# Top-4-of-32 expert layer: results scaled by slot weights and added to a sum in HBM by accumulating scatters; 16 separate slot tables; x joined by products in the last tiles

## The chip, the cores and the metric

One core of one Trainium2 chip runs the whole layer in one launch. The core has TensorE (PE; PEld is its weight load), VectorE (DVE), ScalarE (ACT), GpSimd (POOL) and SyncE (SP). The metric is the device time of one execution in microseconds, the median of several runs.

## The reference

The layer ends in a mixture of experts over 512 latent tokens of 1024 channels. Four of 32 experts are chosen per token and their results are added with softmax weights:

```python
logits = (xf @ lp['router_w'] + lp['router_b']).astype(jnp.float32)
top_v, top_e = lax.top_k(logits, TOP_K)              # TOP_K = 4 of 32
weights = jax.nn.softmax(top_v, axis=-1)
...
gate = xblk @ lp['exp_w_gate'][e] + lp['exp_b_gate'][e]
up = xblk @ lp['exp_w_up'][e] + lp['exp_b_up'][e]
return clamped_swiglu(gate, up) @ lp['exp_w_down'][e] + lp['exp_b_down'][e]
...
contrib = yb[dest] * sorted_w[:, None].astype(yb.dtype)
out = jax.ops.segment_sum(contrib, sorted_tok, num_segments=n_tok)
```

The sum is scaled by a row of modulation values (`ga2`), added to the residual x, and the result goes through a last RMSNorm. All is float32. Before the experts stand the adaLN norm, the input projection, the RWKV and gating branches and their merge; the change leaves these alone but for some instructions that its order puts among them.

## The kernel before

Float32 precision is reached by splitting each operand into a high part (a cast) and a low part (the rest), with three products for one. An expert's three matrices of 1024 x 1024 come in twelve loads of 1 MB (`expert_raw`, on SP, six buffers named raw). ACT casts each to wh (`whigh`), DVE subtracts to wl (`wlow`), and PE runs twelve products of 512 columns on it (`block`). `expert_chain` (line 1625 on) writes this order out by hand for PE, ACT and DVE: per expert r there are 12 positions: 0 to 3 the gate matrix of r, 4 to 7 the down matrix of expert r-1, 8 to 11 the up matrix of r. At each position the cast of the block three further on and the subtraction of the block two further on are written first. SP and POOL take their instructions in the order of the program's text as their scheduler finds them ready.

An expert has 128 slots, about half of them used (512 tokens x 4 / 32 experts = 64 on average). The rows of experts 0 to 3 (`NMM = 4`) are picked by products with one-hot matrices (`gather_x`, two experts at a time: 64 products of 256 columns on PE, 16 casts on ACT). For the later ones `x_rows` gathers 128 rows by an indirect DMA whose list is a column of `slots`, and `x_turn` transposes them. `slots` comes from one table `d_tab` in HBM: `slot_table` sends 16 indirect DMAs from POOL, one per token tile and choice, each of 128 numbers of 4 bytes, all into the same table; then the table is read back. `side` runs this next to expert 0, a piece at each position.

`y_out` (line 1575) copies the expert's result from PSUM to the tile am (one buffer, shared with the next expert's activations) and writes 128 rows to `d_y` from ACT. After the last expert `finish` gathers 16 tiles of rows from `d_y`, and for each token tile adds two of them by products with diagonal weights on PE, the down biases by one more product, the last expert's rows by a one-hot product with `wT`, and two by DVE; then multiplies by `ga2`, adds x, and normalises.

Of the kernel before, what the change touches and what calls it, by code (L numbers as in the profile page):

```python
# [31 lines left out]
NMM = 4  # L32
# [19 lines left out]
NLATE = C_IOTA1 + 128  # L52
# [14 lines left out]
def make_consts():  # L67
# [41 lines left out]
    l[:, C_EB:C_EB + 32] = 1024.0 * np.arange(32)  # L109
    hst = np.zeros((40, 512), np.float32)  # L110
# [41 lines left out]
class K:  # L152
# [1168 lines left out]
    def scratch(self, *shape):  # L1321

        t = self.mraw.tile([128, 2048], F32, name="raw", bufs=RAW)
        n = math.prod(shape)
        names = "abcd"[:len(shape)]
        return t[:, :n].rearrange(f"p ({' '.join(names)}) -> p {' '.join(names)}", **dict(zip(names, shape)))

    def weights(self, pool):
# [7 lines left out]
        yield  # L1336
# [5 lines left out]
        yield  # L1342
        eb = self.late[:, C_EB:C_EB + 32]
        pe = moe.tile([128, 4, 32], F32, name="pe")
        nc.vector.tensor_add(pe, self.pos, eb.rearrange("p (a e) -> p a e", a=1).to_broadcast([128, 4, 32]))
        dst = moe.tile([128, 4, 4], F32, name="dst")
        t = self.scratch(4, 4, 32)
        nc.vector.tensor_mul(t, oh, pe.rearrange("p a (b e) -> p a b e", b=1).to_broadcast([128, 4, 4, 32]))
        nc.vector.tensor_reduce(dst, t, axis=mybir.AxisListType.X, op=OP.add)
        yield  # L1350
        e_ = moe.tile([128, 4, 4], F32, name="dse")
        t = self.scratch(4, 4, 32)
        nc.vector.tensor_mul(t, oh, eb.rearrange("p (a b e) -> p a b e", a=1, b=1).to_broadcast([128, 4, 4, 32]))
# [9 lines left out]
        nc.vector.scalar_tensor_tensor(s, e_, 0.125, f, op0=OP.mult, op1=OP.add)  # L1363
        self.slot = pool.tile([128, 4, 4], I32, name="slot")
        nc.vector.scalar_tensor_tensor(self.slot, big, 8192.0, s, op0=OP.mult, op1=OP.add)
        self.slot_table(pool)
        self.f_, self.e_, self.big = f, e_, big

    def weights_end(self, pool):
# [4 lines left out]
        f, e_, big = self.f_, self.e_, self.big  # L1374
        self.keepR = self.mbL.tile([128, 4096], F32R, name="mL")
        self.keep = self.mb.tile([128, 4096], F32, name="mH")
        wl = moe.tile([128, 4, 4], F32, name="ex")
        nc.vector.tensor_mul(wl, self.wts, oh[:, :, :, NE - 1])
        self.wlast = pool.tile([128, 4, 1], F32, name="wlast")
        nc.vector.tensor_reduce(self.wlast.rearrange("p a b -> p (a b)"), wl, axis=mybir.AxisListType.X, op=OP.add)  # L1380
        yield
        yield from self.down_bias(pool, oh)
        yield
        self.wts2 = pool.tile([128, 4, 4], F32, name="wts2")
        nc.vector.tensor_mul(self.wts2, self.wts, big)
        nc.vector.tensor_sub(self.wts, self.wts, self.wts2)
        yield
        g = moe.tile([128, 4, 4], F32, name="dst")
        nc.vector.tensor_scalar_min(g, f, 127.0)
        self.dsti = pool.tile([128, 4, 4], I32, name="dsti")  # L1390
        nc.vector.scalar_tensor_tensor(g, e_, 0.125, g, op0=OP.mult, op1=OP.add)

        nc.vector.tensor_scalar_min(self.dsti, g, 128.0 * (NE - 1))
        nc.vector.tensor_scalar(g, f, 128.0, -128.0, op0=OP.max, op1=OP.add)
        self.dst2 = pool.tile([128, 4, 4], I32, name="dst2")
        nc.vector.scalar_tensor_tensor(self.dst2, e_, 0.375, g, op0=OP.mult, op1=OP.add)

    def slot_table(self, pool):

        nc = self.nc  # L1400
        tok = pool.tile([128, 4], I32, name="tok")
        lt = self.late[:, C_TOK:C_TOK + 12].rearrange("p (i c) -> p i c", c=3)
        nc.vector.tensor_add(tok.rearrange("p (i c) -> p i c", c=1), lt[:, :, 0:1], lt[:, :, 1:2])
        for i in range(4):
            for k in range(4):
                nc.gpsimd.indirect_dma_start(out=self.d_tab, out_offset=bass.IndirectOffsetOnAxis(ap=self.slot[:, i, k:k + 1], axis=0),  # L1406
                                             in_=tok[:, i:i + 1], in_offset=None, bounds_check=128 * NE - 1, oob_is_err=False)
# [3 lines left out]
    def down_bias(self, pool, oh):  # L1411

        nc = self.nc
        moe = self.moe
        w = self.scratch(4, 3, 32)
        u = self.scratch(4, 4, 32)
# [8 lines left out]
        self.wD = self.keepR[0:96, 0:512].rearrange("p (a b) -> p a b", a=4)  # L1425
        nc.scalar.copy(self.wD, pt)
        nc.vector.tensor_sub(self.wD[32:64], pt[32:64], self.wD[32:64])
        b = self.mraw.tile([96, 2048], F32, name="raw", bufs=RAW)[:, :1024]
        for j in range(3):
            nc.sync.dma_start(b[32 * j:32 * j + 32, :], self.A["exp_b_down"])  # L1430
        yield
        self.bD = self.keepR[0:96, 512:1536]
        nc.scalar.copy(self.bD, b)
        nc.vector.tensor_sub(self.bD[64:96], b[64:96], self.bD[64:96])
# [82 lines left out]
    def x_rows(self, e):  # L1517

        t = self.xg[e] = self.moex.tile([128, 1024], F32, name="xg", bufs=2)
        self.nc.gpsimd.indirect_dma_start(out=t, out_offset=None, in_=self.d_h2, in_offset=bass.IndirectOffsetOnAxis(ap=self.slots[:, e:e + 1], axis=0))  # L1520
# [54 lines left out]
    def y_out(self, E):  # L1575
        y = E["y"] = self.moe.tile([128, 1024], F32, name="am")
        self.nc.scalar.copy(y, E["dn"].rearrange("p a b -> p (a b)"))
        if E["e"] < NE - 1:
            self.nc.scalar.dma_start(self.d_y[128 * E["e"]:128 * E["e"] + 128, :], y)

    def expert_bias(self, tmp, m):
# [20 lines left out]
        zi = tmp.tile([128, 32], I32, name="zi", bufs=1)  # L1602
        nc.gpsimd.memset(zi, 0)
        nc.sync.dma_start(self.d_tab.rearrange("(p e) a -> p (e a)", p=128), zi)

    def experts(self):
# [3 lines left out]
        with self.tc.manual_schedule(engines={ET.PE, ET.Activation, ET.DVE}):  # L1610
            y = self.expert_chain()
        self.finish(y)

    def side(self):

        self.counts(self.small)
        yield
        yield from self.weights(self.small)

    def side_end(self):  # L1620

        yield from self.weights_end(self.small)
        yield from self.last_table()

    def expert_chain(self):
# [29 lines left out]
        gather, side, side_end = iter(()), self.side(), self.side_end()  # L1655
        for i, (r, e, n, pos) in enumerate(seq):
# [5 lines left out]
            if pos == 0 and r % 2 == 1 and r + 1 < NMM:  # L1662
                gather = self.gather_x((r + 1) // 2, xT)

            if pos == 0:
                X = xT.pop(r)
                E["gp"] = ps.tile([128, 2, 512], F32, name="gp", bufs=1)
                if NMM <= r + 2 < NE:
# [9 lines left out]
            elif pos == 4:  # L1678
                P["dn"] = ps.tile([128, 2, 512], F32, name="dn", bufs=1)
                if r == NE:  # L1680
# [4 lines left out]
                    self.up_half(P, 1)  # L1685
            elif pos == (5 if P else 9) and E:
# [22 lines left out]
            if r == 1:  # L1709
                next(gather, None)  # L1710
            next(side if r < 2 else side_end, None)
        self.y_out(P)
        return P["y"]

    def last_table(self):

        nc = self.nc
        z = self.mraw.tile([128, 2048], F32, name="raw", bufs=RAW)[0:1, :1024]
        nc.vector.memset(z, 0.0)
        nc.scalar.dma_start(self.d_y[128 * (NE - 1):128 * (NE - 1) + 1, :], z)  # L1720
        oh = self.scratch(4, 128)
# [25 lines left out]
    def finish(self, y):  # L1747

        nc = self.nc
        yg = {}  # L1750
        for i in range(4):
            for k in range(4):
                if k % 2 == 0:
                    t = self.mraw.tile([128, 2, 1024], F32, name="raw", bufs=RAW)
                yg[i, k] = t[:, k % 2, :]
                nc.gpsimd.indirect_dma_start(out=yg[i, k], out_offset=None, in_=self.d_y, in_offset=bass.IndirectOffsetOnAxis(ap=self.dsti[:, i, k:k + 1], axis=0))
# [292 lines left out]
```

## Time and profile before

| what | value |
|---|---|
| median of 3 runs | 2066.53 us (2059.87 to 2074.01) |
| the profiled execution | 2061.29 us, span 2059.5 us, mean granted TensorE clock 0.964 |
| busy share | PE 95%, DVE 80%, ACT 60%, POOL 16% |
| first block of expert 0 on PE | 830.5 us after the span's start |
| last product of expert 31 | ends at about 2022.5 us |

The span runs from the first to the last instruction of the profiled execution; 1.8 us of its time lie around it. The profiled execution is 5.2 us below the median of the runs. Three stretches matter here: the merge and router up to 821 us, the experts to 2022 us, and the finish. A row of the timeline gives start, duration, engine, line, operation, output<-input; in brackets stands the time the engine sat idle before it, and what released it.

### The profile page before, as it was taken

The numbers are of one execution on the slowest core, as the hardware profiler recorded it, in microseconds if no ns is written. First come the engines' busy times: TensorE is split into PE (matmuls) and PEld (weight loads), VectorE is DVE, ScalarE is ACT, GpSimd is POOL, SyncE is SP. The second block draws the span as 40 slices with busy tenths as digits, with TensorE's granted clock in tenths as the row PEclk, the third lists the DMA queues.
The fourth block names the chain that finished last, engine by engine and source line by source line (L and its number), as shares of the span: only waits on it lengthen the run. The fifth ranks groups of instructions, "written<-read, shape, count | busy, mean of one in ns | idle before, by whom it ended". The sixth has DMA issues, their size and how long they took to land.

```text
span 2059.5 us, 29236 instructions
## 1 busy us (share of the span) xinstructions
PE 1950.5 (95%) x11344; PEld 1523.6 (74%) x11344; DVE 1657.3 (80%) x1760; ACT 1228.1 (60%) x1400; POOL 328.0 (16%) x362
## 2 busy tenths in 40 slices
PE   7999889989999998987999999999999999999986
PEld 4767666766666678876888888888888888888863
DVE  5755876867766367886899999999999999999985
ACT  4522534343534234775777777777777777777762
POOL 0001605343423353122000000000000000000013
PEclk9999988989979998998999999999999999999998
DMA  9666232111112185788999999999999999999994
GB/s 313 210 207 194 62 120 78 45 59 37 46 42 69 39 264 213 292 280 337 355 380 374 390 374 385 371 379 379 373 391 372 382 379 380 379 372 394 362 342 171
DMA packets 154675, 545.11 MB, mean 265 GB/s; under 512 B 14442, under 2 KB 75626, under 8 KB 105379
## 3 DMA queue, kind: packets, MB, share of 16 engines
q1 hardware_dynamic: 140775, 497.97, 65.2%
q0 software_dynamic: 6928, 23.10, 3.3%
q10 hardware_dynamic: 6828, 22.13, 2.7%
q8 instruction: 91, 1.49, 0.3%
q14 instruction: 53, 0.43, 0.1%
HBM read 507.71 MB, written 35.43 MB: 264 GB/s over the span
## 4 chain that ended last, share of the span: by engine, by line
PE 67%; issue 7%; DVE 6%; POOL 3%; DMA 2%; ACT 1%; SPq 0%; POOLq 0%; DVEq 0%; ACTq 0%
PE dn L1490 5%; PE dn L1486 5%; PE dn L1485 5%; PE up L1485 5%; PE gp L1485 5%; PE gp L1486 5%; PE up L1486 5%; PE up L1490 5%; PE gp L1490 5%; PE fill L1079 4%; PE ch L906 1%; PE b L1568 1%; PE mm L865 1%; PE b L1532 1%; POOL d_tab L1406 1%
## 5 line engine op out<-in xcount | busy, mean ns | idle before, releaser
L1474 DVE TENSOR_TENSOR wl<-raw,wh 128x2048 fp32r<-128x2048 f32 x384 | 869.2, 2292 | 52.1 <-PE gp L1490 28.7
L1468 ACT CAST wh<-raw 128x2048 fp32r<-128x2048 f32 x384 | 720.5, 1905 | 96.2 <-PE gp L1486 60.5
L1485 PE MATMUL dn<-wh,aH 128*128 128x512 f32 x512 | 207.6, 406 | 0.4 <-ACT aH L1571 0.4
L1485 PE MATMUL gp<-wh,xH 128*128 128x512 f32 x512 | 204.7, 400 | 0.0
L1485 PE MATMUL up<-wh,xH 128*128 128x512 f32 x512 | 204.5, 399 | 0.0
L1486 PE MATMUL dn<-wh,aL 128*128 128x512 f32 x512 | 202.3, 395 | 1.5 <-DVE aL L1572 1.3
L1486 PE MATMUL gp<-wh,xL 128*128 128x512 f32 x512 | 201.9, 394 | 0.0
L1486 PE MATMUL up<-wh,xL 128*128 128x512 f32 x512 | 201.8, 394 | 0.0
L1520 POOL DMA_INDIRECT xg<-d_h,slots x28 | 26.3, 940 | 898.8 <-PE b L1532 889.4
L1490 PE MATMUL dn<-wl,aH 128*128 128x512 f32 x512 | 140.2, 395 | 0.0
L1490 PE MATMUL up<-wl,xH 128*128 128x512 f32 x512 | 139.2, 393 | 0.0
L1490 PE MATMUL gp<-wl,xH 128*128 128x512 f32 x512 | 139.0, 393 | 0.0
L1571 ACT CAST aH<-b 128x512 fp32r<-128x512 f32 x64 | 37.5, 587 | 133.6 <-PE b L1568 133.6
L1486 PEld LDWEIGHTS dn<-wh,aL 128*128 128x128 f32 x512 | 97.3, 190 | 22.0 <-DVE aL L1572 2.9
L1490 PEld LDWEIGHTS gp<-wl,xH 128*128 128x128 f32 x512 | 96.2, 188 | 22.9
L1490 PEld LDWEIGHTS up<-wl,xH 128*128 128x128 f32 x512 | 96.1, 188 | 22.9
L1486 PEld LDWEIGHTS up<-wh,xL 128*128 128x128 f32 x512 | 96.6, 189 | 21.3
L1490 PEld LDWEIGHTS dn<-wl,aH 128*128 128x128 f32 x512 | 96.6, 189 | 21.2
L1485 PEld LDWEIGHTS dn<-wh,aH 128*128 128x128 f32 x512 | 97.3, 190 | 20.2 <-ACT aH L1571 0.8
L1486 PEld LDWEIGHTS gp<-wh,xL 128*128 128x128 f32 x512 | 96.6, 189 | 21.1
L1485 PEld LDWEIGHTS gp<-wh,xH 128*128 128x128 f32 x512 | 96.4, 188 | 20.7
L1485 PEld LDWEIGHTS up<-wh,xH 128*128 128x128 f32 x512 | 96.4, 188 | 20.7
(510 smaller groups left out, 3753.2 us busy)
## 6 DMA issues: line engine op xcount, KB each, us to landing
raw<-in_exp_w_gate_dram SPq DMA_DIRECT2D x128, 1024.0 KB, 7.2
raw<-in_exp_w_up_dram SPq DMA_DIRECT2D x128, 1024.0 KB, 7.9
raw<-in_exp_w_down_dram SPq DMA_DIRECT2D x128, 1024.0 KB, 9.3
raw<-in_w_ada_dram SPq DMA_DIRECT2D x32, 512.0 KB, 4.5
d_y<-am ACTq DMA_DIRECT2D x31, 512.0 KB, 8.8
raw<-in_w_in_dram SPq DMA_DIRECT2D x24, 512.0 KB, 4.0
wa<-in_w_ada_dram SPq DMA_DIRECT2D x7, 1024.0 KB, 11.7
raw<-in_w_in_dram SPq DMA_DIRECT2D x6, 1024.0 KB, 5.3
```

What stands on the lines that cost most here:

```text
L865: nc.tensor.matmul(mm[:, par, d, :], BK[r, d, ch[d], :], AR[r, d, ch[d], :], start=True, stop=True)
L906: nc.tensor.matmul(sp[:, d, :], bk[:, d, :], uv[:, d, :], start=True, stop=True)
L1079: nc.tensor.matmul(ps, a[:, k, :], b[:, k, :], start=(n == 0), stop=(n == 23))
L1406: nc.gpsimd.indirect_dma_start(out=self.d_tab, out_offset=bass.IndirectOffsetOnAxis(ap=self.slot[:, i, k:k + 1], axis=0), in_=tok[:, i:i + ...
L1468: self.nc.scalar.copy(h, t)
L1474: self.nc.vector.tensor_sub(lo, t, h)
L1485: mm(ps[:, c, :], xH[:, k0 + kk, :], wh[:, cs], start=first and kk == 0, stop=False)
L1486: mm(ps[:, c, :], xL[:, k0 + kk, :], wh[:, cs], start=False, stop=False)
L1490: mm(ps[:, c, :], xH[:, k0 + kk, :], wl[:, cs], start=False, stop=last and kk == 1)
L1520: self.nc.gpsimd.indirect_dma_start(out=t, out_offset=None, in_=self.d_h2, in_offset=bass.IndirectOffsetOnAxis(ap=self.slots[:, e:e + 1], ...
L1532: nc.tensor.transpose(pt[:, j, :], self.xg[e][:, 128 * k:128 * k + 128], self.ident)
L1571: nc.scalar.copy(aH, pt)
```

## The change

Each slot now has a row of two numbers, token + 1 and weight. `places` computes slots and weights at once, ahead of the first two subtractions, and sends 16 indirect DMAs into 16 separate tables; SP and ACT load these in turn, eight each, and `slot_rows` adds them up. The tables are zeroed by 16 POOL DMAs in `expert_bias`; before, one SP DMA did it. `NMM` is 2: experts 2 and 3 are gathered by DMA. `x_rows` skips slots without a token (a bound on the index). `sum_start` writes the weighted down biases to a sum `d_acc` in HBM; `y_out` scales the expert's rows by the slot weights on ACT and adds them to `d_acc` by an indirect DMA with an addition, from POOL; unused slots go to 128 spare rows. `sum_load` reads the sum back after expert 30, `x_sum` adds it to x at the last positions, and `finish` joins x by a product with the unit matrix and the last expert by `wT`, in the hand-written order.

```diff
-NMM = 4
+NMM = 2
+    def places(self, pool):
...            (softmax weights wts, slot number slot, tw = [token + 1, weight])
+        for i in range(4):
+            for k in range(4):
+                nc.gpsimd.indirect_dma_start(out=self.d_tab[4 * i + k], out_offset=bass.IndirectOffsetOnAxis(ap=slot[:, i, k:k + 1], axis=0),
+                                             in_=tw[:, i, k, :], in_offset=None, bounds_check=128 * NE - 1, oob_is_err=False)
+        self.tab = moe.tile([128, 16, NE, 2], F32, name="am")
+        for j, t in enumerate(self.d_tab):
+            (nc.sync, nc.scalar)[j % 2].dma_start(self.tab[:, j], t.rearrange("(s e) a -> s e a", e=NE))
+    def slot_rows(self, pool):
+        v = moe.tile([128, NE, 2], F32, name="slv")
+        nc.vector.tensor_reduce(v, self.tab.rearrange("p j e a -> p e a j"), axis=mybir.AxisListType.X, op=OP.add)
...            (wslot, slots, slotd from v)
-        self.slots = pool.tile([128, NE], I32, name="slots")
-        nc.gpsimd.dma_start(self.slots, self.d_tab.rearrange("(e s) a -> s (e a)", s=128))
+    def sum_start(self, pool):
...            (wD, bD as in down_bias before)
+        for i in range(4):
+            for c in range(2):
+                ps = self.ps.tile([128, 512], F32, name="b1")
+                nc.tensor.matmul(ps, wD[:, i, :], bD[:, 512 * c:512 * c + 512], start=True, stop=True)
+                o = self.keep[:, 2048 + 512 * c:2560 + 512 * c]
+                nc.scalar.copy(o, ps)
+            nc.sync.dma_start(self.d_acc[128 * i:128 * i + 128, :], self.keep[:, 2048:3072])
+            yield
+        nc.sync.dma_start(self.d_acc[NLAT:NLAT + 128, :], self.keep[:, 2048:3072])
     def y_out(self, E):
-        y = E["y"] = self.moe.tile([128, 1024], F32, name="am")
-        self.nc.scalar.copy(y, E["dn"].rearrange("p a b -> p (a b)"))
-        if E["e"] < NE - 1:
-            self.nc.scalar.dma_start(self.d_y[128 * E["e"]:128 * E["e"] + 128, :], y)
+        y = self.moe.tile([128, 1024], F32, name="am")
+        nc.scalar.activation(y, E["dn"].rearrange("p a b -> p (a b)"), AF.Copy, scale=self.wslot[:, e:e + 1])
+        nc.gpsimd.indirect_dma_start(out=self.d_acc, out_offset=bass.IndirectOffsetOnAxis(ap=self.slotd[:, e:e + 1], axis=0), in_=y, in_offset=None, compute_op=OP.add)
-        nc.sync.dma_start(self.d_tab.rearrange("(p e) a -> p (e a)", p=128), zi)
+        for t in self.d_tab:
+            nc.gpsimd.dma_start(t.rearrange("(p e) a -> p (e a)", p=128), zi)
     def expert_chain(self):
...
             high(i)
-            if i:
-                low(i - 1)
+        self.places(self.small)
+        low(0)
+        low(1)
...
+            elif r == NE and pos > 5:
+                self.x_sum(2 * pos - 12)
+                self.x_sum(2 * pos - 11)
...
                 self.y_out(P)
+                if r == NE - 1:
+                    self.sum_load()
+            if r == 1 and pos in (3, 5):
+                self.x_rows(2 + (pos == 5))
-        self.y_out(P)
+        self.finish(P)
+    def sum_load(self):
+        for j in range(2):
+            t = self.mraw.tile([128, 2, 1024], F32, name="raw", bufs=RAW)
+            self.nc.sync.dma_start(t, self.d_acc[256 * j:256 * j + 256, :].rearrange("(i p) d -> p i d", p=128))
+    def x_sum(self, i):
+        self.nc.vector.tensor_mul(self.sums[i], self.sums[i], self.ga2)
+        self.nc.vector.tensor_add(self.xf[i], self.xf[i], self.sums[i])
     def finish
-        (16 indirect gathers of d_y rows; products with diagonal weights, biases, wT; two additions on DVE)
+            nc.vector.tensor_mul(y[:, cs], dn[:, c, :], self.ga2[:, cs])
+                nc.tensor.matmul(ps[:, c, :], self.ident, x[:, cs], start=True, stop=False)
+                nc.tensor.matmul(ps[:, c, :], self.wT[:, i, :], y[:, cs], start=False, stop=True)
+            nc.scalar.activation(o, pf, AF.Square, accum_out=ss)
+            nc.scalar.activation(rs, ss, AF.Sqrt, bias=self.eps[:, 0:1], scale=1.0 / 1024)
+            nc.vector.reciprocal(rs, rs)
+                nc.vector.scalar_tensor_tensor(o[:, cs], pf[:, cs], rs, self.fin[:, cs], op0=OP.mult, op1=OP.mult)
```

ACT ahead of the first expert, before: after the router's `pos` come the third cast, the casts of `gather_x` (xH, xL) and the next block casts.

```order
L1303 COPY pos<-acc 128x128
L1468 CAST wh<-raw 128x2048
L1514 CAST xH<-b_8113 128x256 x2
L1514 CAST xL<-b_8124 128x256 x2
L1514 CAST xH<-b_8135 128x256 x2
L1514 CAST xL<-b_8146 128x256 x2
```

The same place now:

```order
L1306 COPY pos<-acc 128x128
L1480 CAST wh<-raw 128x2048
L1331 ACT_TABLE_LOAD
L1331 ACTIVATE ex<-ex 128x16
L1372 DMA am<-d_tab_69 128x64
L1372 DMA am<-d_tab_71 128x64
L1372 DMA am<-d_tab_73 128x64
L1372 DMA am<-d_tab_75 128x64
L1372 DMA am<-d_tab_77 128x64
L1372 DMA am<-d_tab_79 128x64
L1372 DMA am<-d_tab_81 128x64
L1372 DMA am<-d_tab_83 128x64
L1526 CAST xH<-b_8238 128x256 x2
```

Eight table loads, each of a table that POOL's scatter has to have filled, stand on ACT between the third cast and the casts that hand expert 0 its rows.

POOL in the merge, before (wrL, yaL and mL are low parts of operands of the merge's products, bias that of the expert biases):

```order
L1603 MEMSET zi 128x32
L1599 COPY selz<-first 32x32 x4
L1085 TENSOR_SCALAR gt<-gt 128x512
L1089 TENSOR_TENSOR gt<-gt,ybi 128x512
L185 TENSOR_TENSOR wrL<-raw,wrH 128x4x256
L1601 CAST selE<-selz 128x64
L185 TENSOR_TENSOR yaL<-ya,yaH 128x512
L185 TENSOR_TENSOR wh<-raw,wh 128x1024
L1595 TENSOR_TENSOR bias<-biasf,biash 32x512 x2
L1152 TENSOR_TENSOR mL<-ga,mH 128x512 x8
```

The same place now, up to the first of the thirteen zeroing DMAs in a row:

```order
L1621 DMA d_tab_68<-zi 128x64
L1088 TENSOR_SCALAR gt<-gt 128x512
L1621 DMA d_tab_69<-zi 128x64
L1092 TENSOR_TENSOR gt<-gt,ybi 128x512
L188 TENSOR_TENSOR wrL<-raw,wrH 128x4x256
L1617 CAST selE<-selz 128x64
L1621 DMA d_tab_70<-zi 128x64
L188 TENSOR_TENSOR yaL<-ya,yaH 128x512
L1621 DMA d_tab_71<-zi 128x64
```

Three zeroing DMAs stand ahead of yaL, and thirteen more between yaL and the next wh, bias and mL.

SP at the end, before: after the last expert's up loads come its four down loads.

```order
L1450 DMA raw<-in_exp_w_up_dram 128x2048 x4
L1450 DMA raw<-in_exp_w_down_dram 128x2048 x4
L1737 DMA xH<-d_xn 128x1024
L1737 DMA xL<-d_xn 128x1024
L1798 DMA out_dram<-wh 128x1024 x3
```

The same place now:

```order
L1462 DMA raw<-in_exp_w_up_dram 128x2048 x4
L1462 DMA raw<-in_exp_w_down_dram 128x2048
L1753 DMA xH<-d_xn 128x1024
L1753 DMA xL<-d_xn 128x1024
L1768 DMA raw<-d_acc 128x2x1024 x2
L1462 DMA raw<-in_exp_w_down_dram 128x2048 x3
L1803 DMA out_dram<-wh 128x1024 x3
```

The two loads of the sum, which wait for the scatter of expert 30, stand ahead of the last three down loads of expert 31.

## Rows read from the trace of the kernel before

**Rows 1.** Windows, 1203 to 1240 us: length, busy us per engine, clock, DMA share, GB/s.

```profile
1203.00:1240.00 37.00, 37.00 (x170) 30.20 (x169) 34.58 (x21) 28.30 (x21) 0.94 (x1) 1.00 0.98 378
```

**Rows 2.** Waits of SP, 1000 to 1985 us: us in total, times, longest.

```profile
SPq L1450 <- DVE wl L1474: 850.5, 328, 4.1
```

**Rows 3.** Timeline of ACT ahead of expert 0.

```profile
819.65 1.91 ACT L1468 CAST wh<-raw 128x2048 fp32r<-128x2048 f32 x1
823.32 0.65 ACT L1514 CAST xH<-b 128x256 fp32r<-128x256 f32 x2 [1.76 <-PE b L1511]
```

**Rows 4.** Timeline of PE: first product of expert 0; first piece of the second `gather_x`.

```profile
830.48 0.62 PE L1540 MATMUL gp<-bias,selE 128*128 128x512 f32 x2
...
859.93 1.11 PE L1511 MATMUL b<-xg,mH 128*128 128x256 f32 x8
```

**Rows 5.** Timeline of DVE: the one-hot matrices, then two of the slots' operations.

```profile
819.78 1.23 DVE L1501 TENSOR_TENSOR xg<-late,pm 128x1024 fp32r<-128x1024 f32 x1
...
842.29 0.69 DVE L1348 TENSOR_TENSOR raw<-oh,pe 128x512 f32<-128x512 f32 x1
...
849.35 0.17 DVE L1358 TENSOR_TENSOR dsf<-dst,dse 128x16 f32<-128x16 f32 x1
```

**Rows 6.** Timeline of POOL: first, fourth and last of sixteen scatters into `d_tab`.

```profile
850.39 2.99 POOL L1406 DMA_INDIRECT d_tab<-tok,slot  x1 [31.25 <-DVE tok L1403]
...
871.65 0.97 POOL L1406 DMA_INDIRECT d_tab<-tok,slot  x1 [5.16 <-DMA d_tab<-tok,slot]
...
948.86 2.46 POOL L1406 DMA_INDIRECT d_tab<-tok,slot  x1 [5.26 <-DMA d_tab<-tok,slot]
```

**Rows 7.** Timeline of POOL in the finish: a gather that waits for no other.

```profile
2004.17 0.94 POOL L1756 DMA_INDIRECT raw<-d_y,dsti  x1 [0.30 <-issue]
```

**Rows 8.** Timeline of PE: the first transposes of expert 4's gathered rows.

```profile
972.31 1.09 PE L1532 MATMUL b<-first,xg 128*128 128x128 f32 x4 [11.16 <-DMA xg<-d_h,slots]
```

**Rows 9.** Windows right behind that, columns as in rows 1.

```profile
974.00:978.00 4.00, 4.00 (x11) 3.08 (x10) 2.89 (x2) 2.97 (x3) 0.00 (x0) 0.50 0.08 10
```

**Rows 10.** Timeline of POOL in the merge.

```profile
719.62 1.26 POOL L185 TENSOR_TENSOR yaL<-ya,yaH 128x512 fp32r<-128x512 f32 x1
737.03 2.41 POOL L185 TENSOR_TENSOR wh<-raw,wh 128x1024 fp32r<-128x1024 f32 x1 [16.15 <-ACT wh L1102]
```

**Rows 11.** The tile am: its 31 writes to `d_y`, from issue to landing.

```profile
DMA to landing us min/median/max: 7.5/8.8/10.0
```

**Rows 12.** Timeline of POOL, ACT, DVE: two gathers; am written out, taken again.

```profile
1198.53 0.94 POOL L1520 DMA_INDIRECT xg<-d_h,slots  x1 [35.08 <-PE b L1532]
...
1201.63 0.33 ACTq L1579 DMA_DIRECT2D d_y<-am  x1
...
1213.42 1.10 DVE L1562 SCALAR_TENSOR_TENSOR am<-sg,gg 128x512 f32<-128x512 f32 x1
...
1234.55 0.94 POOL L1520 DMA_INDIRECT xg<-d_h,slots  x1 [35.08 <-PE b L1532]
```

**Rows 13.** Page part 6: loads of 1 MB early in the kernel, median us to landing.

```profile
raw<-in_w_in_dram SPq DMA_DIRECT2D x6, 1024.0 KB, 5.3
```

**Rows 14.** Timeline of the end: expert 30's result, expert 31, and the finish.

```profile
1990.74 1.00 ACT L1577 COPY am<-dn 128x1024 f32<-128x1024 f32 x1
...
2022.49 1.01 ACT L1577 COPY am<-dn 128x1024 f32<-128x1024 f32 x1 [7.69 <-PE dn L1490]
...
2033.03 1.06 ACT L1787 ACTIVATE wh<-xH 128x1024 f32<-128x1024 f32 x1 [1.94 <-DVE xH L1776]
...
2034.20 1.28 ACT L1790 ACT_TABLE_LOAD   x1
...
2037.21 1.88 PE L1766 MATMUL up<-raw,mH 128*128 128x512 f32 x4
...
2047.30 1.27 DVE L1797 SCALAR_TENSOR_TENSOR wh<-xH,rs,mH 128x1024 f32<-128x1024 f32 x1
...
2052.50 1.42 DVE L1797 SCALAR_TENSOR_TENSOR wh<-xL,rs,mH 128x512 f32<-128x512 f32 x2
```

More of the change, by code (lines that the diff above doesn't have):

```diff
@@ new lines, in places @@
+        nc.vector.scalar_tensor_tensor(s, e_, 1.0 / 1024, s, op0=OP.mult, op1=OP.add)
+        slot = pool.tile([128, 4, 4], I32, name="slot")
+        nc.vector.scalar_tensor_tensor(slot, big, 8192.0, s, op0=OP.mult, op1=OP.add)
+        tw = pool.tile([128, 4, 4, 2], F32, name="tw")
+        nc.vector.tensor_copy(tw[:, :, :, 1], self.wts)
+        lt = self.late[:, C_TOK:C_TOK + 12].rearrange("p (i c) -> p i c", c=3)
+        nc.vector.tensor_add(sm, lt[:, :, 0:1], lt[:, :, 1:2])
+        nc.vector.tensor_scalar_add(tw[:, :, :, 0], sm.to_broadcast([128, 4, 4]), 1.0)
@@ L1610, in experts @@
         with self.tc.manual_schedule(engines={ET.PE, ET.Activation, ET.DVE}):
-            y = self.expert_chain()
-        self.finish(y)
+            self.expert_chain()
     def side(self):
+        yield from self.sum_start(self.small)
+        yield from self.slot_rows(self.small)
+        yield
         self.counts(self.small)
         yield
-        yield from self.weights(self.small)
-    def side_end(self):
-        yield from self.weights_end(self.small)
+        self.beyond(self.small)
+        yield
         yield from self.last_table()
@@ L1745, in x_load @@
             nc.sync.dma_start(t, bcast_rows(self.d_mod[3]))
-    def finish(self, y):
-        nc = self.nc
[L1750 to L1756, printed above, removed]
+    def sum_load(self):
+        self.sums = []
+        for j in range(2):
+            t = self.mraw.tile([128, 2, 1024], F32, name="raw", bufs=RAW)
+            self.nc.sync.dma_start(t, self.d_acc[256 * j:256 * j + 256, :].rearrange("(i p) d -> p i d", p=128))
+            self.sums += [t[:, 0, :], t[:, 1, :]]
@@ L1757, in finish @@
+    def x_sum(self, i):
+        self.nc.vector.tensor_mul(self.sums[i], self.sums[i], self.ga2)
+        self.nc.vector.tensor_add(self.xf[i], self.xf[i], self.sums[i])
+    def finish(self, P):
+        nc = self.nc
+        dn = P["dn"]
+        y = self.moe.tile([128, 1024], F32, name="am")
+        for c in range(2):
+            cs = slice(512 * c, 512 * c + 512)
+            nc.vector.tensor_mul(y[:, cs], dn[:, c, :], self.ga2[:, cs])
+        pss = []
         for i in range(4):
             x = self.xf[i]
-            ps = self.ps.tile([128, 2, 512], F32, name=("gp", "up")[i % 2], bufs=1)
@@ L1774, in finish @@
                 cs = slice(1024 // n * c, 1024 // n * (c + 1))
-                nc.vector.tensor_mul(acc[:, cs], acc[:, cs], self.ga2[:, cs])
-                nc.vector.tensor_add(x[:, cs], x[:, cs], acc[:, cs])
-            self.final_norm(i, self.moe, acc, n)
+                nc.vector.scalar_tensor_tensor(o[:, cs], pf[:, cs], rs, self.fin[:, cs], op0=OP.mult, op1=OP.mult)
+                nc.sync.dma_start(self.out[128 * i:128 * i + 128, cs], o[:, cs])
+            pss.append(pf)
+            if i == 0:
+                nc.scalar.copy(x, pf)
+        for i in range(1, 4):
+            nc.scalar.copy(self.xf[i], pss[i])
     def final_norm(self, i, pool, o, n=1):
@@ L1900, in build @@
             self.d_xn = dram.tile([NLAT, 1024], F32, name="d_xn")
-            self.d_y = dram.tile([(NE - 1) * 128 + 1, 1024], F32, name="d_y")
+            self.d_acc = dram.tile([NLAT + 128, 1024], F32, name="d_acc")
             self.d_y2 = dram.tile([NE, 3, 128, 1024], F32, name="d_y2")
-            self.d_tab = dram.tile([NE * 128, 1], I32, name="d_tab")
+            self.d_tab = [dram.tile([128 * NE, 2], F32, name=f"d_tab{j}") for j in range(16)]
             self.d_pm = dram.tile([NE, 128, 4], F32, name="d_pm")
```

171 lines of the change are left out of this document (74 added, 97 removed).

## The prediction

> **What bounds the kernel now.** I read the windows of the expert stretch first. PE is busy for all 37.00 of 37 us at full granted clock, DVE for 34.58, ACT for 28.30 [rows 1]: PE sets the pace, DVE has little to spare. DMA engines show a share of 0.98 at 378 GB/s, but in the waits of SP nearly the whole stretch, 850.5 us, goes to waiting for a buffer that DVE frees [rows 2]. So loads run ahead of need, and a longer transfer costs nothing until that lead is gone. The same row shows a second thing that the whole prediction uses: a DMA instruction whose input isn't ready holds all that stands behind it on its engine.
>
> Where PE isn't at full pace there are four places, read in the timelines: the hand-over to expert 0, the second `gather_x`, one bubble ahead of expert 4, and the end. The change touches all four. The sum is made against the profiled execution (2061.3 us); the median of the runs is 5.2 above it and gets the same difference.
>
> **Part by part.**
>
> *ACT held by the table loads: +34.5 (26 to 61).* Before, ACT casts expert 0's rows from 823.32 on [rows 3] and PE starts expert 0 at 830.48 [rows 4], 7.2 us later. Now eight loads stand between the third cast and these casts, each waiting for a scatter. The scatters need the slot numbers: one-hot matrices end at 819.78 + 1.23 = 821.0; then four wide operations of about 0.7, twelve small ones of 0.2 and a smaller addition [rows 5] take about 5.6: 826.6. Sixteen scatters follow. Before, each waited for the one ahead of it, since all wrote one table: 5.2 us idle, (948.86 - 850.39) / 15 = 6.56 a step [rows 6]. Separate tables end that. A lone step costs POOL 0.94 + 0.30 = 1.24 where nothing is waited for [rows 7], and at most 2.99 + 0.3 [rows 6]; I take 1.6, nearer to the lower, since most issues in rows 6 look like its middle one, 0.97. So the last leaves POOL at 826.9 + 16 x 1.6 = 852.5 and lands 3.6 to 5.6 later (6.56 less 0.97 to 2.99), say 4.5: 857. Then 7.2 us to the first product and 1 for a restart at half clock, which PE shows after 11 us idle [rows 8, 9]: 865 against 830.5. The low end has 1.24 a step, the high end 3.29 a step. SP's eight loads hold the weight loads behind them too; the six buffers are full by then, so I put nothing on that.
>
> *Zeroing from POOL: +4.5 (2 to 17).* Three DMAs stand ahead of yaL (1.26 us itself), 13 more ahead of the next wh, in front of which POOL was idle for 16.15 us [rows 10]. At 1.3 each that gap covers nearly all of the 13; three lie bare (3.9), and a little of the rest. All bare, with some at 1.8, would be 17.
>
> *The second `gather_x` goes: -7.6.* Eight pieces at 0.95 of PE (1.11 with the overlap of its fill) [rows 4].
>
> *The bubble goes: -14.* PE waited 11.16 us for expert 4's rows [rows 8], because the serial scatters ended at 949, and then ran at clock 0.50 till 978 [rows 9], worth about 2.9. Now slots are there 100 us sooner.
>
> *Added for PE: +3.9.* Eight products for `sum_start` (0.23 each, four take at most 1.88 [rows 14]) and the transposes of experts 2 and 3, four pieces of about 0.5.
>
> *The store of the starting sum: +5 (0 to 14).* ACT copies the next token tile into the same buffer that SP's store reads, three times. A store took 7.5 to 10.0 us to land [rows 11]; ACT's copies are a block or more apart, 3.0 us by the 36.02 from one expert's gather to the next [rows 12], so up to some 5 us of each is a hold of ACT, and the casts' lead of three blocks takes most of that.
>
> *The steady stretch: +3 (0 to 200).* The scaling costs ACT what the copy did. But am is one buffer: issued at 1201.63, needed by DVE at 1213.42 [rows 12]: 11.8 us, where a plain write lands in 8.8, 10.0 at most. The scatter adds an issue of 1.24 on POOL [rows 7], so 8.8 becomes 10.0: it fits, barely, if the addition costs under 1.8. That is the value I take; rival A prices the other. The memory traffic grows by a read of 0.5 MB an expert and falls by half a gather: +2%, and SP's lead covers it.
>
> *The end: -5 (-9 to 0).* The finish itself shrinks: before, 37.0 us from the last dn (2022.49) to 2059.5 [rows 14]. Now: scaling y 1.4, four products 1.88, Square 1.06, table load 1.28, root, reciprocal and hand-overs 2, four scalings of 1.27 to 1.42, and 5.6 from the last half's start plus its 1.42 to the end, as before [rows 14]: 18.3. That is 18.7 less. But the last dn comes later. Expert 30's y is ready at 1991.7 [rows 14], its scatter lands at t0, about 1999. SP then loads the sum, 2 MB, and only then the last three down blocks; at 378 GB/s 1 MB takes 2.8 us, with 2.5 of latency (5.3 alone [rows 13]). The second last block is there at t0 + 13.7; cast and subtraction 4.4, which the order places ahead of expert 31's clamp and transposes (5.5), and then four blocks of 3.0: t0 + 35.6, some 2034.5 against 2022.5, and 2 for a stretch at half clock. -18.7 + 12 + 2 = -4.7.
>
> **Sum:** 34.5 + 4.5 - 7.6 - 14 + 3.9 + 5 + 3 - 5 = +24.3. On the profile 2085.6; on the median **2090**.
>
> **Rivals.**
>
> *A: the addition lands too late.* The scatter reads its target before it writes, and no row shows what that costs. If the landing passes the 11.8 us plus the 0.75 that PE leaves DVE, every further us holds gate_mul and with it wl of each of 29 experts. At 2 us late: 58 more, 2148; from 0 (a write's landing plus 1.8) to some 7 (a landing twice as long), 2090 to 2290. For it: the margin is under 2 us and the DMA engines show 0.98. Against it: the data of a plain write, 0.5 MB, is only 1.4 us of its 8.8; a second read of that size still fits. Chance 0.22. The Trainium skill, Collectives: The Full Stack, section The bandwidth ceiling: the fold count and why AG ≠ RS ≠ AR, states that an added transfer has to read two sources, and that reduce-scatter thus gets about half the rate of all-gather. By that the scatter's data time would be 2.8 us and not 1.4, a landing of 11.4 with the issue; if the whole landing halved in rate, rival A's upper end. No run here shows it so far.
>
> *C: scatters cheap, the rest covered.* 1.24 a step and a landing of 3.6: +26; zeroing +2, stores and steady stretch 0, end -6: 26 + 2 - 7.6 - 14 + 3.9 - 6 = +4, 2071. For it: rows 7. Against: all terms at their good ends. Chance 0.25.
>
> *B, not slower: ACT isn't held.* If the eight loads wait outside of ACT's line, its casts go on at 826 and expert 0 starts as before but for 3 us; the sum without the 34.5 and the 5, but with these 3, is -12, 2054. It decides as soon as the hold is under 10 us, where the other terms' -10 meet it. Against it stand rows 2 (SP waits in its line) and the order's eight rows on ACT. Chance 0.07. The opposite, that separate tables don't end the serial steps, would give 16 x 6.56 = 105 of hold and some 2160, chance 0.03.
>
> **From the cases to numbers.** The forecast, 2075 to 2110, has 0.43. The range takes C's value, B's good part left out, and A up to 2 us: 2058 to 2150. 1% (20.7 us) is about what can be told from no change. Faster than 2046 needs B with a good end: 0.05. Within: C, most of B, and the forecast's part under 2087: 0.41. Slower: the rest, 0.54.
>
> **What will show it.** ACT: idle from about 823 to 857 ahead of its am loads, released by d_tab; PE: its first gp product at about 868 and half a clock behind it. POOL: sixteen scatters without waits between them; zeroing DMAs ahead of yaL and wh. No wait for xg before expert 2 or 4. DVE: whether gate_mul waits for the scatter to d_acc; if it does, the period leaves 36.0 and A holds. SP at the end: sum loads waiting for the scatter, down loads behind them, last dn 12 us later relative to expert 31's start, and a finish of 18. If ACT starts expert 0 before 835, or the period changes, I am wrong.

## The result, and the profile after

The changed kernel takes 2149.59 us (median; 2147.65 to 2165.61), against 2067.08 for the kernel before in the same runs: a ratio of 1.041 (95% interval 1.036 to 1.047). It is 82.5 us slower, where about 24 were forecast (the sum says 24.3, its 2090 stands for 2090.8). The profiled execution, 2165.6 us, is the longest of its four, 16 above the median; the stages below are taken from it, span 2163.4 against 2059.5, so they add up to 103.9.

| stage, by PE's first product of an expert | before | now | difference |
|---|---|---|---|
| start to the one-hot matrices (DVE) | 819.8 | 830.5 | +10.7 |
| one-hot matrices to expert 0 | 10.7 | 40.7 | +30.0 |
| expert 0 to expert 4 | 159.8 | 153.1 | -6.7 |
| expert 4 to expert 31, 27 periods | 972.6 (36.02 each) | 1036.6 (38.39 each) | +64.0 |
| expert 31 to the end | 96.6 | 102.5 | +5.9 |

**The expert stretch.** The first fence is the waits of the whole kernel now (engine and line, what it waited for, us in total, times, longest); the second a piece of the timeline of POOL, DVE and PE in one expert; the third what an answer on d_acc says of the scatters (ns: least, median, most; then us from issue to landing).

```profile
DVE am L1576 <- DMA d_acc<-am,slotd: 68.5, 30, 3.1
PE b L1582 <- DVE am L1576: 67.7, 32, 19.4
```

```profile
1590.46 1.03 POOL L1533 DMA_INDIRECT xg<-d_h,slots  x1 [33.18 <-PE b L1546]
1593.91 3.49 POOL L1595 DMA_INDIRECT d_acc<-am,slotd  x1 [2.42 <-ACT am L1594]
...
1607.51 1.06 DVE L1576 SCALAR_TENSOR_TENSOR am<-sg,gg 128x512 f32<-128x512 f32 x1 [2.17 <-DMA d_acc<-am,slotd]
...
1608.72 0.63 PE L1582 MATMUL b<-first,am 128*128 128x128 f32 x4 [1.30 <-DVE am L1576]
```

```profile
L1595 POOL DMA_INDIRECT d_acc<-am,slotd x31: 1544/3491/3496, 943.7 to 2091.4; - x31
...
DMA to landing us min/median/max: 3.8/13.5/14.4
```

A plain write to d_y landed 8.8 us after its issue (median of the ten of 31 whose landing the trace has) [rows 11]; the scatter takes 13.5, of which POOL's issue alone is 3.49. DVE finds am still taken and waits 2.17 us in this expert, PE behind it 1.30; DVE waits so in 30 experts. The operation that waits is `up_half` (line 1576), which writes the activations to am; the prediction and an expectation below call it gate_mul.

The second row of the next fence is a window of about one expert, with the columns of rows 1: PE is no longer full (34.66 of 36). The first row is a stretch behind a longer wait (DVE 3.08 us and PE 2.21, at 1569): the granted clock is 0.62 of full speed, so PE ran most of these 4 us at the lower of its two levels (1.2 and 2.4 GHz).

```profile
1570.00:1574.00 4.00, 4.00 (x14) 3.14 (x13) 4.00 (x4) 3.60 (x3) 0.00 (x0) 0.62 0.78 258
1600.00:1636.00 36.00, 34.66 (x157) 27.58 (x156) 31.93 (x20) 25.72 (x19) 4.53 (x2) 1.00 0.98 356
```

The waits account for the whole +64.0. In each of the 22 periods at full clock the period is 36.19 us (that of the run with a tile of its own, below) plus DVE's wait, less 0.33 to 0.36 us that the order absorbs. Over the 27 periods the waits are 62.8 us, of which some 9.2 are absorbed; five periods at the lower clock, 39.9 to 40.1 us long, add 1.2 each beyond their waits; and 4.5 are the step from 36.02 to 36.19: 64.1 in all. In three other runs below that leave the scatter as it is, with two such periods or none, the stretch is 54.4 to 59.2 us longer than before.

**The hand-over to expert 0.** These are rows of DVE, POOL, ACT and PE in the changed kernel; they answer to [rows 3 to 6].

```profile
830.46 1.23 DVE L1513 TENSOR_TENSOR xg<-late,pm 128x1024 fp32r<-128x1024 f32 x1
...
836.29 6.69 DVE L1486 TENSOR_TENSOR wl<-raw,wh 128x2048 fp32r<-128x2048 f32 x3
836.68 2.83 POOL L1368 DMA_INDIRECT d_tab<-tw,slot  x1 [6.86 <-DVE tw L1365]
839.81 1.83 POOL L1368 DMA_INDIRECT d_tab<-tw,slot  x1 [0.30 <-issue]
841.95 1.87 POOL L1368 DMA_INDIRECT d_tab<-tw,slot  x1 [0.30 <-issue]
844.13 0.97 POOL L1368 DMA_INDIRECT d_tab<-tw,slot  x1 [0.30 <-issue]
...
859.42 0.97 POOL L1368 DMA_INDIRECT d_tab<-tw,slot  x1 [0.30 <-issue]
862.65 0.65 ACT L1526 CAST xH<-b 128x256 fp32r<-128x256 f32 x2 [28.90 <-DMA d_tab<-tw,slot]
871.15 0.63 PE L1554 MATMUL gp<-bias,selE 128*128 128x512 f32 x2
```

Sixteen scatters now follow each other in 23.7 us, 1.48 each, and ACT stands 28.90 us in front of its loads. The bubble ahead of expert 4 [rows 8] is gone: 37.6 us from expert 3 to 4, not 50.1.

**The end.** Rows of POOL, SP, ACT, PE and DVE behind expert 30's result; they answer to [rows 14].

```profile
2091.39 1.54 POOL L1595 DMA_INDIRECT d_acc<-am,slotd  x1 [31.55 <-ACT am L1594]
2097.64 0.89 SPq L1768 DMA_DIRECT2D raw<-d_acc  x2
2098.63 1.50 SPq L1462 DMA_DIRECT2D raw<-in_exp_w_down_dram  x3
2107.75 1.90 ACT L1480 CAST wh<-raw 128x2048 fp32r<-128x2048 f32 x1 [16.64 <-DMA raw<-in_exp_w_down_dram]
2116.85 1.09 PE L1582 MATMUL b<-first,am 128*128 128x128 f32 x4 [19.37 <-DVE am L1576]
...
2138.46 2.08 PE L1791 MATMUL gp<-am,mH 128*128 128x512 f32 x2 [4.54 <-DVE am L1783]
```

The last three down loads leave SP behind the sum's loads, which left when the scatter had landed; ACT waits 16.64 us for them, PE 19.37. From the last dn product's end (2133.1) on, 30.3 us remain: 0.9 of products with x, 4.5 more of waiting for x_sum, then the finish, which starts at the lower clock (0.50 in this window, columns of rows 1):

```profile
2138.00:2144.00 6.00, 5.54 (x7) 2.44 (x8) 1.00 (x2) 0.02 (x1) 0.00 (x0) 0.50 0.00 0
```

### The profile page after: what moved, and what is told of

It is laid out like the page before. It is cut to its first block, busy times and chain, and to the rows that moved or that the text cites. A ratio compares the mean times of both kernels' runs of the same rounds, so it can differ in the third digit from the quotient of the medians.

```text
span 2163.4 us, 29257 instructions
## 1 busy us (share of the span) xinstructions
PE 1974.8 (91%) x11280; PEld 1523.8 (70%) x11280; DVE 1650.5 (76%) x1761; ACT 1227.0 (57%) x1387; POOL 417.1 (19%) x392
## 4 chain that ended last, share of the span: by engine, by line
issue 45%; POOL 6%; PE 5%; DMA 4%; DVE 1%; ACT 0%; POOLq 0%; SPq 0%; ACTq 0%; DVEq 0%
POOL d_acc L1595 4%; DMA d_acc<-am,slotd 3%; POOL xg L1533 1%; PE dn L1498 1%; PE dn L1502 1%; PE dn L1497 1%; DMA raw<-in_exp_w_down_dram 1%; PE up L1498 0%; PE up L1497 0%; PE b L1582 0%; PE gp L1791 0%; DVE am L1576 0%; POOL d_tab L1368 0%; DVE raw L1773 0%; DMA xg<-d_h,slots 0%
## 5 line engine op out<-in xcount | busy, mean ns | idle before, releaser
L1480 ACT CAST wh<-raw 128x2048 fp32r<-128x2048 f32 x384 | 722.0, 1905 | 108.0 <-PE gp L1498 72.2
L1533 POOL DMA_INDIRECT xg<-d_h,slots x30 | 33.2, 1105 | 924.4 <-PE b L1546 848.7
L1497 PE MATMUL gp<-wh,xH 128*128 128x512 f32 x512 | 209.5, 409 | 0.0
L1498 PE MATMUL gp<-wh,xL 128*128 128x512 f32 x512 | 206.9, 404 | 0.0
L1585 ACT CAST aH<-b 128x512 fp32r<-128x512 f32 x64 | 37.6, 588 | 199.5 <-PE b L1582 199.5
L1595 POOL DMA_INDIRECT d_acc<-am,slotd x31 | 106.0, 3420 | 169.0 <-ACT am L1594 169.0
L1576 DVE SCALAR_TENSOR_TENSOR am<-sg,gg 128x512 f32<-128x512 f32 x64 | 69.1, 1079 | 68.6 <-DMA d_acc<-am,slotd 68.5
```

The lines of the kernel that those rows point to most:

```text
L1480: self.nc.scalar.copy(h, t)
L1497: mm(ps[:, c, :], xH[:, k0 + kk, :], wh[:, cs], start=first and kk == 0, stop=False)
L1498: mm(ps[:, c, :], xL[:, k0 + kk, :], wh[:, cs], start=False, stop=False)
L1576: self.nc.vector.scalar_tensor_tensor(E["a"][:, 4 * h:4 * h + 4, :], v4(E["u"]), 1.0, v4(E["gg"]), op0=OP.add, op1=OP.mult)
L1585: nc.scalar.copy(aH, pt)
L1595: nc.gpsimd.indirect_dma_start(out=self.d_acc, out_offset=bass.IndirectOffsetOnAxis(ap=self.slotd[:, e:e + 1], axis=0), in_=y, in_offset=N ...
```

## The experiments

Each is the changed kernel with one edit, but for the two sums of edits. Periods are the mean of the 27 from expert 4 to 31. Totals are medians; the ratio is to the kernel before in the same runs.

| run | total us | ratio (95%) | expert 0 at | period | expert 31 to end |
|---|---|---|---|---|---|
| changed kernel | 2149.6 | 1.041 (1.036 to 1.047) | 871.2 | 38.39 | 102.5 |
| e1_y_own | 2096.1 | 1.014 (1.009 to 1.020) | 870.7 | 36.19 | 101.0 |
| e2_no_add | 2095.5 | 1.014 (1.012 to 1.016) | 866.9 | 36.33 | 97.5 |
| e8_y_early | 2096.7 | 1.014 (1.009 to 1.019) | 866.9 | 36.21 | 101.0 |
| e3_pool_loads | 2133.6 | 1.032 (1.029 to 1.035) | 833.9 | 38.22 | 101.7 |
| e4_sum_late | 2145.6 | 1.037 (1.034 to 1.041) | 877.2 | 38.07 | 87.8 |
| e7_zero_sp | 2152.6 | 1.041 (1.038 to 1.044) | 867.8 | 38.04 | 103.6 |
| e5_three | 2058.5 | 0.997 (0.994 to 1.000) | 834.3 | 36.19 | 85.8 |
| e6_best | 2047.1 | 0.991 (0.989 to 0.994) | 836.2 | 36.23 | 82.3 |

**A tile of its own for the scaled result.**

```diff
-        y = self.moe.tile([128, 1024], F32, name="am")
+        y = self.moe.tile([128, 1024], F32, name="yo")
```

> The scaled result has a tile of its own; the activations' tile am no longer waits for the scatter. Theory (DVE's gate_mul waits for am, PE behind it): DVE's 68 us of waiting for the scatter go, an expert takes 36.0 to 36.3 us and not 38.4, total about 2085 (2080 to 2095). Rival (the scatter's extra reads take DMA time from the weight loads): the period stays near 38.4 and the total near 2148; ACT's casts wait for raw instead. Rival (POOL's 3.49 us per scatter slow DVE or PE): period between, over 37.5.

The period falls from 38.39 to 36.19 and no period is longer than 36.2; 53.5 us go from the total. The scatter moves as much and POOL issues it for as long (3.49 us), so neither the traffic nor POOL costs more than the 0.17 us that are left over 36.02 (what these are stays open). The total is 11 above the expected 2085 and 1 above its range: that number took the waits of the profiled execution, 16 us above its median, off the median. Between the two profiled executions it is 66.1 us (2163.4 to 2097.3). Whether the other executions of the changed kernel waited less isn't shown.

**The scatter without its addition.**

```diff
-    ..., in_=y, in_offset=None, compute_op=OP.add)
+    ..., in_=y, in_offset=None)
```

> The scatter writes its rows without the addition (so the sum over experts is left out); all waits stay. If the addition is what makes the scatter land late: landing 9 to 10.5 us and not 13.5, POOL's issue nearer to 1 us than to 3.5, DVE waits under 15 us in all, total 2085 to 2100. If it is the indirect issue from POOL: landing over 12, waits of 60 us and more, total 2140 to 2150.

DVE's waits fall to 9.2 us in 18 experts, the period to 36.33. One of those is in the timelines of POOL and DVE of this run:

```profile
1520.44 2.89 POOL L1595 DMA_INDIRECT d_acc<-am,slotd  x1 [2.44 <-ACT am L1594]
...
1532.80 1.08 DVE L1576 SCALAR_TENSOR_TENSOR am<-sg,gg 128x512 f32<-128x512 f32 x1 [0.93 <-DMA d_acc<-am,slotd]
```

In these 18 experts am comes free only 11.6 to 13.1 us after the issue began (12.36 here); in the others it was free when DVE asked for it, at 11.4. So even without the addition am comes free at 11.6 us in the median, on the edge of what the order leaves. The total and the waits are those of the first expectation, but the issue and the landing are not: the indirect issue from POOL, 2.9 us and not about 1, takes up the margin, and the addition, some 2 us more (0.6 of it in the issue), goes beyond it.

**The scaled result one position earlier.**

```diff
-                if 4 <= r + 2 < NE:
-                    self.x_rows(r + 2)
...
             elif pos == 8:
...
-            elif pos == 9:
-                self.y_out(P)
+                if P:
+                    self.y_out(P)
+                    if 4 <= r + 2 < NE:
+                        self.x_rows(r + 2)
```

> No tile added: the scaled result is written one position earlier in the order (about 3 us), and the gather of the expert after next behind its scatter on POOL. Theory (am comes free 2.3 us too late, by a margin): the scatter starts 3 to 4 us earlier, DVE's waits for it fall from 68 us to under 15, an expert takes 36.2 to 36.6 us, total 2085 to 2105. Rival (the addition's landing lengthens with what it overlaps): period over 37.5, total over 2125. On POOL's 3.49 us per scatter: if the issue waits for the end of the subtraction that DVE is in, each scatter ends 1.5 us behind the end of that operation, whatever its length; if it is the issue's own work, it stays 3.5 us.

Without a byte of memory added the waits for the scatter fall to 3.1 us and the period to 36.21. In most experts the scatter still stands behind a gather on POOL and starts only 2.1 us nearer to it (1.34 us from start to start, 3.45 in the changed kernel); that is enough, the margin was that thin. On the issue's length the run does decide. Most of its scatters meet DVE's subtraction in nearly the same phase as before (3.40 us), but the first three and the last three meet it later and take 1.54 to 2.41 us; all 31 end 1.4 to 1.5 us behind the end of the subtraction. That is the first reading of the expectation (rows in the last section).

**Table loads from POOL.**

```diff
-            (nc.sync, nc.scalar)[j % 2].dma_start(self.tab[:, j], ...)
+            nc.gpsimd.dma_start(self.tab[:, j], ...)
```

> All sixteen table loads are issued from POOL behind the scatters; ACT and SP don't wait for them. Theory (ACT is held from 833 to 862): expert 0's first product comes 26 to 30 us earlier after the one-hot matrices, total 2149.6 - 28 = about 2122 (2116 to 2130). Rival (the hold only hides a wait that is needed anyway): PE then waits for the rows of expert 2, total 2140 or more.

The hold goes: from the one-hot matrices to expert 0 it is 11.2 us, not 40.7. But the rival has a share: expert 1 lasts 60.2 us against 48.7, since DVE, in its order, waits for the last table ahead of expert 0's activations, and PE 14.80 us behind it. These are rows of DVE and PE of this run.

```profile
879.19 1.87 DVE L1379 TENSOR_REDUCE slv<-am 128x64 f32<-128x1024 f32 x1 [8.94 <-DMA am<-d_tab]
...
886.30 1.11 PE L1582 MATMUL b<-first,am 128*128 128x128 f32 x4 [14.80 <-DVE am L1576]
```

By expert 4, 18.7 of the 29.5 us are left (counted from the one-hot matrices), and the total is 16 lower, between the two expectations.

**The sum's loads behind the down loads.**

```diff
-                if r == NE - 1:
-                    self.sum_load()
...
                 if r == NE:
+                    self.sum_load()
                     self.x_load(1)
```

> The two loads of the sum are written behind the last expert's down loads. Theory (three down blocks wait 16.6 us behind the sum on SP's line): ACT's wait of 16.6 us for raw and PE's of 19.4 go, the stretch from expert 31's first product to the end falls from 102.5 to 87 to 92 us, total about 2137 (2134 to 2142). Rival (the sum itself is then late): x_sum waits as long, total over 2145.

The end shrinks by 14.7 us, to 87.8, as its mechanism said; PE's wait of 19.37 is 4.76 here. The total, 4 us lower and 4 above its range, doesn't show it: this profile reaches expert 0 6 us later than the changed kernel's, ahead of anything that the edit touches, and this run's totals scatter by 11 us. It is where the rival put it (over 2145), but the rival's reason isn't: the wait ahead of the finish is 4.5 us, as before the edit.

**Zeroing from SP.**

```diff
-            nc.gpsimd.dma_start(t.rearrange("(p e) a -> p (e a)", p=128), zi)
+            nc.sync.dma_start(t.rearrange("(p e) a -> p (e a)", p=128), zi)
```

> The sixteen zeroing DMAs go out from SP, not POOL. Theory (the merge lost some 4.6 us to POOL's zeroing): from POOL's last FS of the merge to expert 0's one-hot matrices 4 to 5 us less; the total falls by as much, less than runs scatter. Rival (POOL's zeroing was covered): no change there, or weight loads late behind SP's sixteen.

From the start of POOL's last pair of FS operations to the one-hot matrices it takes 119.7 us, against 120.5 in the changed kernel, 117.2 to 120.6 in the other seven runs, with POOL's zeroing, and 115.4 in the kernel before. So POOL's zeroing isn't shown to be the cause. That the merge became some 2 to 5 us longer is seen in every run; why stays open.

**Three edits together, and two more.** The first takes the own tile, POOL's loads and the late sum. The second also puts the tables in a free part of another tile, adds them up three positions later, and moves x_sum ahead:

```diff
+        self.tab = self.keep[:, 3072:4096].rearrange("p (j e a) -> p j e a", j=16, a=2)
...
-        yield from self.slot_rows(self.small)
         self.counts(self.small)
         yield
         self.beyond(self.small)
+        yield
+        yield
+        yield from self.slot_rows(self.small)
...
                     self.up_half(P, 1)
+                    self.x_sum(0)
+                    self.x_sum(1)
-            elif r == NE and pos > 5:
-                self.x_sum(2 * pos - 12)
-                self.x_sum(2 * pos - 11)
+            elif r == NE and pos == 6:
+                self.x_sum(2)
+                self.x_sum(3)
```

> The three edits together: own tile for the scaled result, table loads from POOL, sum loads behind the down loads. If the three losses are separate places of one chain they add up: 2149.6 less 2.2 x 27 = 59, less 26 (what the earlier expert 0 left by expert 4), less 14.7 at the end: about 2050 (2042 to 2056), 0.7% under the kernel before. Rival (another resource bounds the expert stretch once the waits are gone): over 2065.

> As the three together, with the table loads in a free part of another tile and their addition three positions later, so that PE doesn't idle 15 us in expert 1 for the slots, and x_sum two positions earlier: another 8 to 16 us less, about 2038 (2030 to 2046). If the slots are simply late for expert 2's gather, the idle time moves to expert 2's transposes and no more than 5 us come off.

By stages the losses are separate links: with the three edits the period is that of the own tile (36.19), the end 85.8 us where the late sum alone has 87.8, and expert 0 starts as with POOL's loads. 91 us come off with three edits, 102.5 with all; the medians of the three single runs (53.5, 16.0 and 4.0) would have given 74. The first is 0.3% under the kernel before (0.0 to 0.6%); the second, 2047.1 us, is 0.9% faster than it (0.6 to 1.1%). Both are 8 to 9 us above their numbers, and 2.5 and 1 above their ranges. In the second, expert 1 takes 49.4 us and not 58.4, and of PE's waits for slots one of 3.38 us is left, ahead of expert 2's transposes; the wait for x_sum ahead of the finish falls from 4.53 to 1.09. Rows of PE in that run:

```profile
895.42 1.06 PE L1546 MATMUL b<-first,xg 128*128 128x128 f32 x4 [3.38 <-DMA xg<-d_h,slots]
...
2023.76 1.12 PE L1793 MATMUL gp<-am,mH 128*128 128x512 f32 x2 [1.09 <-DVE am L1785]
```

## Why the prediction was wrong

**The step that failed** is the steady stretch: +3, with the reason that the scatter "fits, barely, if the addition costs under 1.8". It measured +64. The mechanism stood there as rival A, with its place and its condition, at 0.22 and with 2148 us; it is what happened. The mistake is one of price: the scatter's issue was taken as 1.24 from a gather on an otherwise idle core [rows 7], while the first scatter of the kernel before, 2.99 us, and the last, 2.46 [rows 6], stood in the list of rows as the higher bound and were used in the hold alone. Had the issue been priced at 2.99 here, the landing would have been at 11.8 us without any addition, at the budget itself, and A would have been the likeliest case. The own tile, the dropped addition and the earlier write each take the stretch back to 36.2 or 36.3.

What the runs showed in its place is a release of 13.5 us against the 11.4 at which DVE asks for am. It is made of 2.0 us of the issue's wait for a subtraction on DVE (last section), 0.9 of the issue itself, 0.6 that the addition puts on it, and 10.0 from the issue's end to the landing, against 8.8 without the addition. The addition alone, 1.9, is thus near the 1.8 allowed; the issue's 2.0 of waiting was not in the sum at all. A's condition, "11.8 us plus the 0.75", has no row for its 0.75; measured are 11.4 and 0.34.

The wait could be read beforehand. The prediction says of rows 6 that most issues look like the 0.97; in the whole trace five of the sixteen do, and the mean is 1.74. Ten take 1.2 to 3.0 us, and each of these ends 0.8 to 1.1 us behind the end of the DVE operation that it started in. This row of DVE in the kernel before goes with the last of rows 6 (948.86 to 951.32):

```profile
948.18 2.30 DVE L1474 TENSOR_TENSOR wl<-raw,wh 128x2048 fp32r<-128x2048 f32 x1
```

That A's total comes within 2 us of the median is partly luck. On the profiled execution, from which the terms are made, A's sum is +82 and the stages add up to +104; that execution lies 16 us above its median, and four of the other parts of the sum are off by 4 to 11 us.

**ACT held:** the mechanism was right. +30.0 from the one-hot matrices to expert 0 against 34.5; the step of 1.48 us (three of 2.1 to 3.1, and 1.27 from then on) lies next to the 1.6 chosen, and 8.5 us follow from the first cast to the first product, where 8.2 were put. The load edit takes it away.

**Zeroing, +4.5:** the stretch of the merge grew by 5.1 in this profile, but moving the DMAs to SP didn't give it back. The term has the right size and no shown cause. The other 5.6 us of +10.7 lie ahead of the first zeroing DMA; in the nine profiles with changes the one-hot matrices start anywhere from 822.6 to 836.3, against 819.8 in the one before, so they may be scatter.

**Second gather, bubble, added products, stores, in sum -12.7:** -6.7 on the profile. Two of these four periods (expert 2 to 4) already hold the scatter's wait, some 2.4 each in the rest of the kernel; with the own tile, which has no such wait, it is -11.2 (148.6 against 159.8).

**The end, -5:** +5.9. The late last dn was right: 72.2 us from expert 31's first product, against 59.6, so 12.6 later, where 14 were put. The finish was mis-sized: 30.3 us from the last dn, not 18.3 (whose terms, as listed, add up to 18.45). x_sum's eight operations (9.7 us on DVE) stand between the last subtraction and y, which the forecast leaves out: some 4 us. Square starts 5.5 us after the first products behind that wait, where 1.9 and a hand-over were put, mostly since they run at the lower clock (the window under The end). And 9.3 us pass from the first scaling to the last, where three scalings in a row, 3.8, were put: DVE waits 4.6 in between for the roots of the other tiles.

**Rivals B and C:** ACT was held by its loads, against B; the scatters took 1.48 us and not C's 1.24, and C's quiet steady stretch isn't what happened.

The Trainium skill, Collectives: The Full Stack, section The bandwidth ceiling: the fold count and why AG ≠ RS ≠ AR, was drawn on in rival A: an addition reads two sources. By it the prediction put 1.4 us more for the scatter's data, or a landing of twice the length. The runs are near the first: from the issue's end to the landing it is 10.0 us with the addition and 8.8 without it. That the second read is what costs this isn't shown.

## What to carry to other kernels

When a buffer's plain write is turned into an indirect one from another engine, its release has to be budgeted anew, as issue, landing and addition, from the dearest row of such an issue, or from what makes it dear (here, what DVE was doing at that moment), and held against the time at which the buffer is taken again; a budget of 11.8 us with 1.8 to spare is a wait until shown otherwise. A load or store that waits for far work must not stand in the line of an engine that hands out near work: here ACT stood 28.90 us before its loads and SP's down loads behind the sum's. Where one buffer is what everybody waits for, a second tile, or writing it one position earlier, gave back as much as dropping the operation.

## What the runs showed of the hardware that was not expected

An indirect DMA on POOL waits for the subtraction that DVE is in. In the rows of the hand-over above, DVE's three subtractions start at 836.29 and end at 838.6, 840.8 and 843.0. The three scatters issued meanwhile end at 839.51, 841.64 and 843.82, each 0.8 to 1.0 us behind one of these ends; from 844.13 on, with DVE idle, each takes 0.97. In the run with POOL's loads DVE went on subtracting (ACT wasn't held), and its scatters kept changing length. Rows of POOL and DVE of that run:

```profile
835.91 1.11 DVE L1405 TENSOR_REDUCE mH<-mH 128x128 f32<-128x512 f32 x1
836.43 0.97 POOL L1368 DMA_INDIRECT d_tab<-tw,slot  x1 [0.30 <-issue]
837.44 2.27 DVE L1486 TENSOR_TENSOR wl<-raw,wh 128x2048 fp32r<-128x2048 f32 x1
837.70 2.85 POOL L1368 DMA_INDIRECT d_tab<-tw,slot  x1 [0.30 <-issue]
...
841.92 2.29 DVE L1486 TENSOR_TENSOR wl<-raw,wh 128x2048 fp32r<-128x2048 f32 x1
842.13 2.92 POOL L1368 DMA_INDIRECT d_tab<-tw,slot  x1 [0.30 <-issue]
...
866.50 4.38 POOL L1372 DMA_DIRECT2D am<-d_tab  x8 [0.26 <-DMA am<-d_tab]
867.96 2.29 DVE L1486 TENSOR_TENSOR wl<-raw,wh 128x2048 fp32r<-128x2048 f32 x1 [5.96 <-ACT wh L1480]
```

The two that start just behind the start of a subtraction take 2.85 and 2.92, and end 0.84 behind its end. The one of 836.43, which starts in a sum over one input, isn't held. Nor are the plain DMAs: the eight table loads from 866.50 on go out in 0.55 us each, four of them while a subtraction of the same kind runs.

The scatter of an expert's rows does the same, 1.46 us behind the end of the subtraction. These rows of DVE and POOL are of the run with the earlier write: the first scatter starts just before the second subtraction's end (971.39), the other 0.31 us into the first of three (which ends at 1047.8).

```profile
966.91 4.48 DVE L1486 TENSOR_TENSOR wl<-raw,wh 128x2048 fp32r<-128x2048 f32 x2
971.17 1.69 POOL L1595 DMA_INDIRECT d_acc<-am,slotd  x1 [31.01 <-ACT am L1594]
...
1045.53 6.70 DVE L1486 TENSOR_TENSOR wl<-raw,wh 128x2048 fp32r<-128x2048 f32 x3
1045.84 3.46 POOL L1595 DMA_INDIRECT d_acc<-am,slotd  x1 [0.30 <-issue]
```

In the changed kernel the last scatter takes 1.54 us (2091.39 above), 0.08 us before the end of a subtraction, and those of the stretch 3.49, where they start 0.25 us or so into one: about 2.0 of the 3.49 us are this wait. In the run with the earlier write the first three, short, scatters land 11.0 to 12.2 us after their start; those from 1045 to 1960, all but one of them 3.2 to 3.5 us long, have a median of 13.3.

The landing depends on more than the issue: the last scatter of the changed kernel, with SP's weight loads held back (a DMA share of 0.50 from 2091 to 2098), lands 6.1 us after its start, 4.6 behind its issue, against 10.0 in the stretch beside a share of 0.98. That the traffic is the reason wasn't tried apart.

The Trainium skill, SBUF — State Buffer, section Who interferes with whom, says that DMAs issued from GpSimd can be held up by a DVE operation that has the port pair the two share, and lets tensor_tensor out of that, as an inference, since it takes only the read side. For the plain DMAs above the trace agrees; for the indirect ones it differs: what holds up these scatters is tensor_tensor with two inputs in SBUF. The same section also says that a DVE instruction with two SBUF inputs contends with a GpSimd instruction that reads SBUF. That would cover them if the issue reads its list of rows there; whether that is the reason wasn't tried.
